# Attention in a hybrid layer: six heads' probabilities turned by VectorE's 32x32 transposes and a DRAM scratch, with gates beside them in single PSUM banks

## The chip, the cores and the metric

The kernel runs on one core of a Trainium2 chip, as one launch. The metric is the device time of the whole kernel in microseconds (us). The engines are named as the profile names them: PE (TensorE, the matrix engine; PEld are its weight loads), DVE (VectorE), ACT (ScalarE), POOL (GpSimd) and SP (SyncE, which here only issues DMAs).

## The reference

One layer over 16 meta tokens and 512 tokens (528 in all) of width 1024: half an FFN, a mixer, half an FFN, a last norm. The mixer adds retention (4 heads) and an attention with selected keys (8 heads of 128), each behind a sigmoid gate. The change lies in the attention and beside it; cut to that, with `selected` standing for a mask that an index of its own makes:

```python
u = rmsnorm(h, mix_norm)
proj = u @ w_in                                  # ..., aq, ak, av, ..., g_ret, g_att
aq = rope(aq.reshape(B, T, 8, 128), pos)
ak = rope(ak.reshape(B, T, 8, 128), pos)
av = av.reshape(B, T, 8, 128)
s = einsum('bqhd,bkhd->bhqk', aq, ak) * 128 ** -0.5
p = softmax(where(selected | meta_and_causal, s, -inf), axis=-1)
ya = einsum('bhqk,bkhd->bqhd', p, av).reshape(B, T, 1024) @ w_att_out
merged = sigmoid(g_ret) * yr + sigmoid(g_att) * ya
h = h + merged @ w_mix_out
```

All is float32.

## The kernel before

**Numbers in two parts.** PE multiplies fp32r operands. A float32 tensor is kept as a high and a low half: `split` (L115 to L118) has ACT copy the high half (L117) and DVE subtract it from the source for the low half (L118). A product is three matmuls, high by high, high by low, low by high (`mm3`, L157). Weights are fetched as `raw` by SP (L133, two buffers) and split into `whi` and `wlo` (three buffers each): a split can start when PE has done with the weights three before.

**Layout.** Activations lie feature by token: 128 features in the partitions, tokens along the free dimension. Scores of one head (`score`, L1964) come query by key: four blocks `prob[j]` of 128 queries in the partitions, with the meta keys and the first 128(j + 1) keys in the free dimension. DVE adds the mask and takes the maximum (L1967), ACT takes the exponential and its sum (L1970), DVE scales to one (`to_one`, L1974 and L1975, tile `pj`). The values are multiplied with the probabilities key by query, so the blocks have to be turned.

**Turning, before.** `transpose_p` has PE transpose the 128x128 blocks with the identity into PSUM (tile `psPT`, 13 blocks at L1988 and a 16-key tail at L1990) and splits each of four key blocks into `pth` and `ptl`. Columns begin at `KQ[kb]`, 512, 400, 272 and 256 of them. `split_rows` makes the tail's stacked rows (`ptail`). `weigh_v` runs 13 matmuls into `psao` (L1536, L1537) and splits the result into the head's part of `vo`.

**The loop over heads.** An iteration h is scores(h), then `proj_q` and `proj_k` of head h + 1 (tiles `psaq`, `psak`; rope by `rope_swap`, whose multiply by sin is POOL's, L1294), the transposes of head h, one gate of 24 matmuls (`wide_gate`: a retention gate, `psgate`, or an attention gate, `psga`, which goes to the DRAM scratch `gd`), and the weighing of head h. Scores of head 0 lie ahead of the loop. Head 7 has no next head, and runs two more gates in that place.

**Order.** Each engine works through its instructions in order. On the engines in `BUSY`, stretches under `manual_schedule` keep the order written; elsewhere a planner with a cost for each instruction sets the order on each engine. DMAs issued by SP, ACT and POOL stand in the queue of that engine among its other instructions. A DMA that waits for data holds what is behind it.

**PSUM.** Single banks come from `sm_tile`, pairs of banks from `mm_tile`. A new tile waits until the last reader of the one that had the place is done.

**Norms.** The sum of squares over features needs a sum over partitions. `folded` adds the upper half of the partitions to the lower and splits; `sum_columns` (L225) multiplies with ones; `rstd_of` takes POOL's power (L252), DVE places the result on diagonals (L283), PE spreads it over the partitions (L266), ACT copies that to SBUF (L267). For the retention heads the same is done by `fold`, `norm_sums`, `norm_diag` and `norm_all` (L1587), hung into other work: `proj(..., ((6, f), ...))` calls f ahead of the sixth weight row's matmuls. `pick(n)` issues n steps of the index selection.

## Time and profile before

| | us |
|---|---|
| median of 3 runs (1516.49 to 1516.9) | 1516.57 |
| the profiled execution, whole | 1517.2 |
| its span, first to last instruction | 1515.4 |

In a row of the profile's timeline stand the start and the duration in us, the engine, the line, the operation, output and inputs by the program's names, the shape, and how many instructions the row joins; in brackets the idle time before it and what ended that. A group row gives the line, the engine, the operation, the shapes and the count, then the busy time in us and the mean in ns, then the idle time before it. A DMA row gives the target, the source, the issuing queue, the count, the KB of each, and the median us from issue to landing. A table of stretches gives the busy us and instruction count of each engine between two times.

### The profile page before, as it was taken

To read this page: it belongs to the slowest core of one execution; us is meant where nothing else is said; L and a number is where in the kernel's file an instruction comes from. 1 tells how busy PE (TensorE), PEld (TensorE's weight loads), DVE (VectorE), ACT (ScalarE), POOL (GpSimd) and SP (SyncE) were. 2 spreads that over 40 slices of the span, in tenths; PEclk is the share of its full clock that TensorE was granted. 3 is DMA by queue.
4 is the path that set the end of the run, shared out by engine and by line. 5 is a ranking of instruction groups with operands and counts; after the bars stand their busy time and mean duration, and the time that the engine had idled before them with its cause. 6 is when DMAs were issued, how large, how long until landed. Compare 5 with 4: busy or idle time off the path is not lost. (4 is left out here: it accounts for less than half of the span.)

```text
span 1515.4 us, 23886 instructions
## 1 busy us (share of the span) xinstructions
PE 1505.2 (99%) x9748; PEld 1368.3 (90%) x9748; DVE 1100.8 (73%) x1710; ACT 727.7 (48%) x1134; POOL 103.2 (7%) x135
## 2 busy tenths in 40 slices
PE   9999999999999999999999999999999999999997
PEld 8999999999988888888888889998888899899996
DVE  4988585786786768678888887665455888586675
ACT  5655263454354444443333357666345445254453
POOL 1000000003101120000000131110001000000000
PEclk9999999999999999999999999999999999999999
DMA  5132323226544444232323242333443223233232
GB/s 169 61 118 89 116 92 112 87 95 202 201 157 162 166 149 151 87 122 86 120 75 97 89 133 75 91 86 105 146 145 113 84 84 112 83 112 112 84 124 85
DMA packets 151741, 173.48 MB, mean 114 GB/s; under 512 B 4944, under 2 KB 123240, under 8 KB 150992
## 3 DMA queue, kind: packets, MB, share of 16 engines
q1 hardware_dynamic: 142992, 151.58, 31.2%
q0 software_dynamic: 3808, 11.38, 2.0%
q10 hardware_dynamic: 4832, 9.00, 1.7%
q8 instruction: 76, 1.25, 0.3%
q14 instruction: 33, 0.27, 0.1%
HBM read 155.94 MB, written 16.01 MB: 113 GB/s over the span
## 5 line engine op out<-in xcount | busy, mean ns | idle before, releaser
L328 ACT ACTIVATE whi<-raw 128x1024 fp32r<-128x1024 f32 (+2 forms) x184 | 169.5, 924 | 128.3 <-PE psd L157 41.6
L329 DVE TENSOR_TENSOR wlo<-raw,whi 128x1024 fp32r<-128x1024 f32 (+2 forms) x184 | 198.5, 1083 | 40.3 <-ACT whi L328 40.3
L157 PE MATMUL psqX<-th,whi 128*128 128x264 f32 (+1 forms) x432 | 122.3, 283 | 0.1
L157 PE MATMUL psqX<-tl,whi 128*128 128x264 f32 (+1 forms) x432 | 122.3, 283 | 0.0
L157 PE MATMUL psqX<-th,wlo 128*128 128x264 f32 (+1 forms) x432 | 122.2, 283 | 0.0
L118 DVE TENSOR_TENSOR wlo<-raw,whi 128x1024 fp32r<-128x1024 f32 (+1 forms) x60 | 73.6, 1226 | 52.1 <-ACT whi L117 51.2
L328 ACT ACTIVATE whi<-wsum 128x1024 fp32r<-128x1024 f32 x72 | 76.3, 1060 | 70.4 <-PE psd L2187 22.0
L117 ACT ACTIVATE whi<-raw 128x1024 fp32r<-128x1024 f32 (+1 forms) x60 | 62.4, 1044 | 85.9 <-PE psat L157 26.6
L329 DVE TENSOR_TENSOR wlo<-wsum,whi 128x1024 fp32r<-128x1024 f32 x72 | 87.8, 1220 | 12.5 <-ACT whi L328 12.5
L157 PEld LDWEIGHTS psqX<-th,whi 128*128 128x128 f32 x432 | 82.1, 190 | 0.4 <-DVE g L544 0.4
L157 PEld LDWEIGHTS psqX<-th,wlo 128*128 128x128 f32 x432 | 82.0, 190 | 0.0
L157 PEld LDWEIGHTS psqX<-tl,whi 128*128 128x128 f32 x432 | 82.0, 190 | 0.0
L157 PE MATMUL psro<-vo,whi 128*128 128x512 f32 x256 | 79.2, 390 | 0.2 <-DVE vo L329 0.2
L157 PE MATMUL psd<-hl,whi 128*128 128x264 f32 x352 | 71.3, 284 | 0.0
L157 PE MATMUL psd<-hh,wlo 128*128 128x264 f32 x352 | 70.7, 283 | 0.0
L157 PE MATMUL psd<-hh,whi 128*128 128x264 f32 x352 | 70.7, 282 | 0.0
L2187 PE MATMUL psd<-wlo,hh 128*128 128x512 f32 (+1 forms) x182 | 69.2, 382 | 0.0
L2187 PE MATMUL psd<-whi,hh 128*128 128x512 f32 (+1 forms) x182 | 69.2, 382 | 0.0
L2187 PE MATMUL psd<-whi,hl 128*128 128x512 f32 (+1 forms) x182 | 69.2, 382 | 0.0
L157 PEld LDWEIGHTS psro<-vo,whi 128*128 128x128 f32 x256 | 48.0, 188 | 10.7 <-DVE vo L329 0.5
L157 PEld LDWEIGHTS psd<-hh,wlo 128*128 128x128 f32 x352 | 54.4, 188 | 0.0
L157 PEld LDWEIGHTS psd<-hh,whi 128*128 128x128 f32 x352 | 54.1, 188 | 0.0
(460 smaller groups left out, 4517.0 us busy)
## 6 DMA issues: line engine op xcount, KB each, us to landing
raw<-in_ffn_w_up_dram SPq DMA_DIRECT2D x22, 1024.0 KB, 5.0
raw<-in_ffn_w_gate_dram SPq DMA_DIRECT2D x21, 1024.0 KB, 5.0
raw<-in_w_in_dram SPq DMA_DIRECT2D x18, 1024.0 KB, 5.0
raw<-in_w_in_dram SPq DMA_DIRECT2D x33, 512.0 KB, 3.5
raw<-in_ffn_w_down_dram SPq DMA_DIRECT2D x24, 512.0 KB, 4.4
w<-in_w_in_dram SPq DMA_DIRECT2D x24, 512.0 KB, 6.9
raw<-in_ffn_w_down_dram SPq DMA_DIRECT2D x12, 768.0 KB, 4.4
raw<-in_w_ret_out_dram SPq DMA_DIRECT2D x8, 1024.0 KB, 4.8
```

The source lines that it names most:

```text
L117: nc.scalar.activation(hi, src, AF.Copy)
L118: eng.tensor_tensor(lo, src, hi.bitcast(F32), ALU.subtract)
L157: nc.tensor.matmul(o, a[:, k, :], b[:, sl], start=first and k == 0 and i == 0, stop=last and k == nk - 1 and i == 2, skip_group_check=onto)
L328: nc.scalar.activation(hi, src, AF.Copy)
L329: return lambda: nc.vector.tensor_tensor(lo, src, hi.bitcast(F32), ALU.subtract)
L2187: nc.tensor.matmul(ps, a[:, bs], m[:, j, cs], start=first and i == 0, stop=last and i == 2)
```

## The change

Heads 1 to 6 no longer use `transpose_p`.

- `turn(h)`: DVE's transpose works on 32x32 squares. Four of them (416, 288, 160 and 512 columns) write the squares of the four blocks to `cross`, and a fifth the 16-key tail to `crosst`. POOL then issues four DMAs to a DRAM scratch `pd` (1 MB a head, two of them in turn), each for 32 partitions: 512 pieces of 512 B, 256 KB. A small DMA takes the tail to `land4`.
- `turned(h)`: SP issues four DMAs from `pd` to `land0` to `land3`, key by query, of 512, 512, 384 and 256 columns: 256, 256, 192 and 128 KB.
- `turned_parts`: the splits into `pth` and `ptl`, now from SBUF.
- `weigh_turned`: the 13 matmuls over 512, 512, 384 and 256 columns; the queries come out in another order, which the last split puts right. It runs one iteration later than before, after the next head's `proj_k`. Iteration 1 therefore weighs no head, and head 6 is weighed in iteration 7.

Beside these heads the gate takes a single bank. The values of heads 4 to 7 are split in iteration 0 (after head 0's weighing) rather than 1, and the tail values of those heads are placed in iteration 4 rather than 3. The `tmp` buffers go from seven to four; `cross` takes the room of the values' raw buffer. For the last retention head `fold` moves from after the second to after the first of two gates, `norm_sums` from the sixth to the fourth weight row of `psak`, and two `pick` calls change. The last norm's column sums take an `mm_tile`, its spread an `sm_tile`.

```diff
--- before.py
+++ after.py
@@ -225,13 +225,12 @@
             nc.tensor.matmul(col[:, 2 * b : 2 * b + 2], f[:, b * P : (b + 1) * P], ones_r[:, :2], start=True, stop=True)
         return col[:, :8].rearrange("p (b j) -> p b j", j=2)[:, :, 0]
 
-    def rstd_folded(ssum, dim, dst, sp, psum):
+    def rstd_folded(ssum, dim, dst, sp, place, psum):
 
         f = tmp().bitcast(F32R)[:, :S]
         for _ in folded(ssum, f, tmp()[:, :S]):
             pass
-        col = psum()
-        yield from rstd_of(sum_columns(f, col), S, dim, dst, sp, psum, P)
+        yield from rstd_of(sum_columns(f, place()), S, dim, dst, sp, psum, P)
 
     def rstd_steps(ssum, n, dim, dst, sp, psum, apart=False):
 
@@ -308,6 +307,8 @@
+    pd = dpool.tile([2, S, 4, P], F32, name="pd")
 
     def gap(p, n):
 
@@ -1819,12 +1820,11 @@
             keep_gate(ps)
             weigh(p, 2)
             weigh(p, 3)
-            pick(1)
+            fold(p)
 
         def last_1(ps):
             keep_gate(ps)
-            fold(p)
-            pick(1)
+            pick(2)
 
         def last_2(ps):
             first_kq.append(ps)
@@ -1839,7 +1839,7 @@
             n = 4 - (h == p)
             more += queries_keys(h) + gates[:n] + outputs(h - 1, beside_outputs(h - 1)) + gates[n:]
         more += steps_of(tiles("gr", w_in, OFF_GR + 2 * P, 2), [proj("psgate", REAL, (), last_0), proj("psgate", REAL, (), last_1)])
-        more += steps_of(tiles("ak", w_in, OFF_AK, 1), [proj("psak", None, ((6, lambda: norm_sums(p)), (7, lambda: norm_diag(p))), last_2)])
+        more += steps_of(tiles("ak", w_in, OFF_AK, 1), [proj("psak", None, ((4, lambda: norm_sums(p)), (7, lambda: norm_diag(p))), last_2)])
         more += steps_of(tiles("aq", w_in, OFF_AQ, 1), [proj("psaq", REAL, ((2, lambda: norm_all(p)), (4, lambda: two_normed_parts(p, 0)), (6, lambda: two_normed_parts(p, 2))), last_3)])
         more += outputs(p, lambda i: pick(2 + (i == 0)))
         more += steps_of(tiles("gr4", w_in, OFF_GR + 4 * P, 1), [proj("psgate", REAL, (), first_kq.append)])
@@ -1906,21 +1906,27 @@
         nc.scalar.activation(t, ps, AF.Sigmoid)
         return t
 
+    crs = ExitStack()
     with pool("ao") as ao:
         vo = [ao.tile([P, AH, S], F32R, tag=f"vo{i}", name="vo") for i in range(2)]
         ao_parts = [(vo[0][:, c, :], vo[1][:, c, :]) for c in range(AH)]
         with pool("at") as at:
-            tp.update(pool=at, bufs=7)
+            tp.update(pool=at, bufs=4)
             cos, sin = rope_tables(1, at)
             gap(at, 32)
             prob = []
             for j in range(4):
-                wj = min(P * (j + 2), T)
+                wj = min(P * (j + 2), T + NM)
                 pj = at.tile([P, wj], F32, tag=f"pj{j}", name=f"pj{j}")
-                if j < 3:
-                    nc.gpsimd.memset(pj[:, NM + P * (j + 1) :], 0.0)
+                nc.gpsimd.memset(pj[:, NM + P * (j + 1) :], 0.0)
                 prob.append(pj)
-            gap(at, 48)
+
+
+            Q0 = [0, 0, P, 2 * P]
+            land = [at.tile([P, S - q0], F32, tag=f"land{kb}", name=f"land{kb}") for kb, q0 in enumerate(Q0)]
+            land.append(at.tile([NM, NM], F32, tag="land4", name="land4"))
+            crosst = at.tile([P, 32], F32, tag="crosst", name="crosst")
+            gap(at, 32)
             tails(at, 64)
             gap(at, 16)
             cq, ck = (Cols(w_in, o_ + P, AH - 1, step=1) for o_ in (OFF_AQ, OFF_AK))
@@ -1980,6 +1986,49 @@
                 for j in (2, 1, 0, 3):
                     score(j, q, k)()
 
+            def part_tiles(kb, n):
+                return [at.tile([P, S - Q0[kb]], F32R, tag=f"pt{c}{kb}", name=f"pt{c}")[:, :n] for c in "hl"]
+
+            def turn(h):
+
+                for j in (2, 1, 0, 3):
+                    m = min(-(-(NM + P * (j + 1)) // 32), 16)
+                    nc.vector.transpose(cross[:, :m, j, :], prob[j][:, : 32 * m].rearrange("p (b k) -> p b k", k=32))
+                nc.vector.transpose(crosst, prob[3][:, S : S + 32])
+                d = pd[h % 2]
+                for a in range(4):
+                    nc.gpsimd.dma_start(d.rearrange("(b i) a c -> a i b c", i=32)[a],
+                                        cross[32 * a : 32 * a + 32].rearrange("p b j c -> p b (j c)"))
+                nc.gpsimd.dma_start(land[4], crosst[96 : 96 + NM, NM:])
+
+            def turned(h):
+                for kb, q0 in enumerate(Q0):
+                    nc.sync.dma_start(land[kb].rearrange("p (a c) -> p a c", a=4),
+                                      pd[h % 2, kb * P : (kb + 1) * P, :, q0 // 4 :])
+
+            def turned_parts():
+                parts = []
+                for kb, q0 in enumerate(Q0):
+                    ph, pl = part_tiles(kb, S - q0)
+                    split(land[kb], ph, pl)
+                    parts.append((ph, pl))
+                split_rows(land[4], tp["p"][:, :NM], "hlh")
+                return parts
+
+            def weigh_turned(h, parts, v):
+
+                ps = mm_tile("psao")[:, :S]
+                for kb, q0 in enumerate(Q0):
+                    vh, vl = (part[:, kb * P : (kb + 1) * P] for part in v[:2])
+                    ph, pl = (part.rearrange("p (a c) -> p a c", a=4) for part in parts[kb])
+                    o = ps.rearrange("p (a c) -> p a c", a=4)[:, :, q0 // 4 :]
+                    if q0 == 0:
+                        (ph, pl), o = parts[kb], ps
+                    for i, (a, b) in enumerate(((vh, ph), (vh, pl), (vl, ph))):
+                        nc.tensor.matmul(o, a, b, start=kb == 0 and i == 0, stop=False)
+                nc.tensor.matmul(ps[:, KQ[4] :], v[2], tp["p"][:TR, :NM], start=False, stop=True)
+                split(*(t.rearrange(f"p ({o}) -> p a j c", a=4, j=4) for o, t in zip(("a j c", "j a c", "j a c"), (ps, *ao_parts[h]))))
+
             def transpose_p():
                 parts = []
                 for kb in range(4):
@@ -1989,8 +2038,7 @@
                     if kb == 3:
                         nc.tensor.transpose(ps[:NM, 0:P], prob[3][:, 4 * P : T], ident)
                     n = S - KQ[kb]
-                    ph = at.tile([P, wide(n)], F32R, tag=f"pth{kb}", name="pth")[:, :n]
-                    pl = at.tile([P, wide(n)], F32R, tag=f"ptl{kb}", name="ptl")[:, :n]
+                    ph, pl = part_tiles(kb, n)
                     if kb == 3:
                         split_rows(ps[:NM, P - NM : P], tp["p"][:, :NM], "hlh")
                     split(ps[:, KQ[kb] :], ph, pl)
@@ -2004,7 +2052,7 @@
 
             def wide_gate(tile=None):
                 if gr.at < gr.n:
-                    gate_acc(KD - gr.n + gr.at, gate(gr, at, wide=True))
+                    gate_acc(KD - gr.n + gr.at, gate(gr, at, wide=tile is None))
                 else:
                     t = gate_a(tile or mm_tile("psga")[:, :S])
                     nc.sync.dma_start(gd[KD + ga.at - 1], t)
@@ -2025,6 +2073,7 @@
                     to_one()
                 vs = split_values(raw, [v[:, :4, :] for v in vo])
                 raw = fetch_values(5, vraw())
+            pend = None
             for h in range(AH):
                 more = h + 1 < AH
                 if h:
@@ -2034,17 +2083,30 @@
                 else:
                     wide_gate(sm_tile("psga"))
                     wide_gate()
-                pt = transpose_p()
-                wide_gate()
-                weigh_v(h, pt, vs[h])
-                if h == 1:
+                if pend is not None:
+                    weigh_turned(h - 1, pend, vs[h - 1])
+                    pend = None
+                if h == 0:
                     with tc.manual_schedule(engines=BUSY):
-                        more_vs = split_values(raw, [v[:, 4:, :] for v in vo])
-                if h == 3:
+                        vs += split_values(raw, [v[:, 4:, :] for v in vo])
+                    vrs.close()
+                    crp = crs.enter_context(pool("cross", 1, side="right"))
+                    cross = crp.tile([P, 16, 4, 32], F32, tag="cross", name="cross")
+                    for j in range(3):
+                        nc.gpsimd.memset(cross[:, 4 * j + 5 :, j, :], 0.0)
+                if 0 < h and more:
+                    turn(h)
+                    wide_gate(sm_tile("psga"))
+                    turned(h)
+                    pend = turned_parts()
+                else:
+                    pt = transpose_p()
+                    wide_gate()
+                    weigh_v(h, pt, vs[h])
+                if h == 4:
                     place_tails(5)
-                    vs += more_vs
-
-        vrs.close()
+
+        crs.close()
 
         mgs = ExitStack()
         mgp = mgs.enter_context(pool("mgp", 1, side="right"))
@@ -2112,7 +2174,7 @@
         RS = slice(0, S)
 
 
-        norm = rstd_folded(ssum3, D, R3, ou, lambda: mm_tile("psn")[:, :S])
+        norm = rstd_folded(ssum3, D, R3, ou, lambda: mm_tile("psn"), lambda: sm_tile("psn"))
         raw0 = load_w(wg2[:, 0 : 2 * P], KD, 2 * P)
         ps0 = [sm_tile("psg") for _ in range(2)]
         for i in range(2):
```

## The prediction

> **What bounds the kernel now.** I read the page's busy shares first, then its chain of waits.
>
> ```profile
> span 1515.4 us, 23886 instructions
> ...
> PE 1505.2 (99%) x9748; PEld 1368.3 (90%) x9748; DVE 1100.8 (73%) x1710; ACT 727.7 (48%) x1134; POOL 103.2 (7%) x135
> ...
> PE 42%; DVE 0%; ACT 0%; issue 0%; POOL 0%; POOLq 0%
> ```
>
> PE works 1505.2 of 1515.4 us, and only PE has a share of the chain that ended last. So the time changes by PE work taken off or added, and by waits put between PE instructions; work on DVE, ACT, POOL and the queues counts only where PE comes to wait for it. Next, the stretches of the attention loop, one head each (PE, PEld, DVE, ACT, POOL, clock, DMA share, GB/s), head 2's and the sum of six:
>
> ```profile
> 936.60:958.90 22.30, 22.30 (x141) 20.26 (x140) 14.56 (x36) 14.73 (x28) 3.92 (x3) 1.00 0.26 72
> ...
> sum 133.90, PE 133.90 PEld 121.57 DVE 88.63 ACT 88.32 POOL 20.58; mean PE 22.32 PEld 20.26 DVE 14.77 ACT 14.72 POOL 3.43
> ```
>
> PE is full at 22.3 us a head. DVE and ACT have over 7 us free, POOL 18, the DMA engines about two thirds. There the change puts its new work.
>
> **Off PE: the transposes.** The timeline shows PE at the end of head 1's loads of k, the 14 transposes, and the gate after them. A matmul's duration overlaps the next one, so I count from start to start.
>
> ```profile
> 927.62 1.58 PE L1988 MATMUL psPT<-ident,pj 128*128 128x128 f32 x13
> ...
> 929.06 0.48 PE L157 MATMUL psgate<-xh,whi 128*128 128x512 f32 x1
> ...
> 929.38 0.39 PE L157 MATMUL psgate<-xl,whi 128*128 128x512 f32 x1
> ...
> 929.61 0.39 PE L157 MATMUL psgate<-xh,wlo 128*128 128x512 f32 x1
> ```
>
> 927.62 to 929.06 is 1.44 us for the transposes, and the first gate matmul takes 0.32 instead of 0.23, so 1.53 us a head. Heads 0 and 7 keep theirs: 6 x 1.53 = 9.2 us off PE. The PSUM bank use of L1988 goes with them.
>
> **Onto PE: wider weighing.** The turned weighing has as many matmuls (13), over 512, 512, 384 and 256 columns in place of 512, 400, 272 and 256.
>
> ```profile
> 934.62 0.39 PE L1536 MATMUL psao<-pth,vo 128*128 128x512 f32 x1
> ...
> 934.85 0.39 PE L1536 MATMUL psao<-ptl,vo 128*128 128x512 f32 x1
> ...
> 935.48 0.34 PE L1536 MATMUL psao<-ptl,vo 128*128 128x400 f32 x1
> ...
> 935.66 0.47 PE L1536 MATMUL psao<-pth,vo 128*128 128x400 f32 x2
> ...
> 935.97 0.29 PE L1536 MATMUL psao<-ptl,vo 128*128 128x272 f32 x1
> ...
> 936.10 0.41 PE L1536 MATMUL psao<-pth,vo 128*128 128x272 f32 x2
> ...
> 936.34 0.28 PE L1536 MATMUL psao<-ptl,vo 128*128 128x256 f32 x1
> ...
> 936.61 0.43 PE L1964 MATMUL psS<-ak,aq 128*128 128x400 f32 x1
> ```
>
> Starts lie 0.23 us apart at 512 columns, 0.18 at 400, 0.13 at 272; 384 columns come between the last two, about 0.175. Three matmuls each: 3 x (0.05 + 0.045) = 0.28 us a head, 6 x 0.28 = 1.7 us. The other PE work only changes places: a turned head is weighed in the next iteration, after the next head's k.
>
> **Two new waits.** In the built programs' instruction order I compared, for every PE instruction, how many PE instructions lie between it and the latest one that its inputs go back to. At two places the change puts a weight split, which waits for a gate's last matmul, ahead of work that PE needs at once. The rows that price them are head 1's in ACT and DVE order:
>
> ```profile
> 932.12 0.65 ACT L117 ACTIVATE ak<-tmp 128x528 fp32r<-128x528 f32 x1 [0.66 <-DVE tmp L1295]
> ...
> 932.83 0.70 DVE L118 TENSOR_TENSOR ak<-tmp,ak 128x528 fp32r<-128x528 f32 x1
> ...
> 933.82 0.38 ACT L117 ACTIVATE pth<-psPT 128x256 fp32r<-128x256 f32 x1 [1.06 <-DVE ptail L1370]
> ...
> 934.24 0.42 DVE L118 TENSOR_TENSOR ptl<-psPT,pth 128x256 fp32r<-128x256 f32 x1 [0.51 <-ACT pth L117]
> ...
> 934.64 1.06 ACT L117 ACTIVATE whi<-raw 128x1024 fp32r<-128x1024 f32 x1 [0.44 <-PE psgate L157]
> ...
> 935.74 1.23 DVE L118 TENSOR_TENSOR wlo<-raw,whi 128x1024 fp32r<-128x1024 f32 x1 [1.07 <-ACT whi L117]
> ```
>
> Before, the halves of k (ak) and of the last probability block (pth, ptl) are made first; then whi starts 0.02 us after PE has left the gate (934.62), and wlo after it.
>
> (1) Iteration 1. It has no head to weigh, so scores(2) follow gate(1) directly, and ACT now has whi ahead of ak's high half, DVE wlo ahead of its low half. From the gate's end whi runs to +1.08, wlo to +2.35, ak's low half to +3.08. The first score matmul needs the high half alone and covers 0.18: a stall of 2.9 us. Queued behind whi on ACT are the sigmoid and all of softmax(2); PE meanwhile has proj_q(3) and proj_k(3), so nothing else is late.
>
> (2) Iteration 0. Head 0 is not turned, but its last block's pth and ptl now stand behind the same pair: whi to +1.08, wlo to +2.35, ptl to +2.8. The weighing reaches that ptl 1.72 us after its start (936.34 - 934.62): a stall of 1.1 us. Before, that weighing took
>
> ```profile
> 912.12 0.39 PE L1536 MATMUL psao<-pth,vo 128*128 128x512 f32 x1
> ...
> 914.28 1.90 PE L1964 MATMUL psS<-ak,aq 128*128 128x400 f32 x12
> ```
>
> 2.16 us, against head 1's 1.99: 0.17 of waiting is there already, so +0.9. Both together cost +3.8 us; the bounds are 0 (the gate's weights freed in time after all) and 6 (a splitting pair more in front).
>
> **The last norm.** rstd_folded's column sums move to an mm bank and its spread to an sm bank. Now:
>
> ```profile
> 1172.30 0.40 PE L266 MATMUL psn<-tmp,ones_r 128*128 128x512 f32 x1
> ...
> 1172.74 0.60 ACT L267 ACTIVATE R<-psn 128x512 f32<-128x512 f32 x1 [4.90 <-PE psn L266]
> ...
> 1173.39 0.50 PE L157 MATMUL psu<-xh,whi 128*128 128x512 f32 x1 [0.69 <-ACT R L267]
> ...
> 1173.73 0.39 PE L157 MATMUL psu<-xl,whi 128*128 128x512 f32 x1
> ```
>
> psu waits until ACT has emptied the bank: it starts 1.09 us after psn rather than 0.23, and its second matmul comes 0.34 later rather than 0.23. In the new order psu doesn't depend on that copy: -1.0 us; bounds -1.0 and 0. The fold in last_0 and the earlier norm_sums move DVE and ACT work of the last retention head forward by a step; no PE work changes, PE's weights there are loaded ahead, and I take 0, within -0.3 and +0.5 (bounds: an ACT or DVE piece as long as ak's low half, 0.70, less what covers it).
>
> **The trip and its cover.** Per turned head DVE gets five 32x32 transposes of 1408 columns; nothing like it is in the trace. By wlo's 1.2 ns a column it's 1.7 us (bounds: 0.8 and 3.4, half and double). DVE then is busy 16.3 us of some 21: hidden. POOL gets five issues, SP four:
>
> ```profile
> L1126 POOL DMA_DIRECT2D vst<-part x12 | 8.5, 712 | 77.8 <-DVE part L1154 59.9 <-ACT part L1202 10.9 <-DVE part L1192 6.9
> ```
>
> ```profile
> q1 hardware_dynamic: 142992, 151.58, 31.2%
> ...
> vst<-part POOLq DMA_DIRECT2D x12, 512.0 KB, 5.4
> ...
> sa<-gd ACTq DMA_DIRECT2D x8, 256.0 KB, 4.0
> ...
> vraw<-vst SPq DMA_DIRECT2D x4, 256.0 KB, 15.1
> ...
> vd<-rest POOLq DMA_DIRECT2D x6, 128.0 KB, 2.1
> ...
> rqk<-fs SPq DMA_DIRECT2D x2, 256.0 KB, 5.6
> ```
>
> vst has as many pieces (512, of 1 KB) as one write of pd (of 512 B): 0.71 us to issue, so five take 3.6 of POOL's 18 free. Landing: 2.1 (vd) to 5.4 (vst). Now the times, from the start of a head's scores (936.61 for head 1's next, 914.28 for head 0's next):
>
> ```profile
> 930.01 1.33 POOL L1294 TENSOR_TENSOR tmp<-tmp,sin 128x528 f32<-128x528 f32 x1 [4.50 <-ACT tmp L1292]
> ...
> 942.00 0.49 DVE L1975 TENSOR_SCALAR pj<-pj,stat 128x528 f32<-128x528 f32 x1
> ```
>
> Probabilities are final at +5.9 (942.49 - 936.61), turned at about +8. Of the four writes the last stands behind k's rope multiply on POOL, which ends at +17.1 (931.34 - 914.28) less the 1.5 of transposes: issued by +16.3, landed by +18.4 to +21.7. SP then loads 256, 256, 192 and 128 KB: two to three loads' time of 4.0 to 5.6, so +26 to +31; DVE's low halves (0.7 each at 512 columns) are done 1 to 2 us later. PE weighs that head after the next head's k, one period (21.0) plus 13.3 (927.62 - 914.28) = +34.3. So 1 to 6 us to spare: I cost it at 0. If the cover is gone, each us late is a us of PE in each of six heads.
>
> [...]
>
> **Sum.** -9.2 + 1.7 + 2.9 + 0.9 - 1.0 = -4.7 us: span 1515.4 to 1510.7. The profiled run took 1517.2, 1.8 more than its span; the median of the three runs is 1516.57, which I take as the start: 1511.9.
>
> **Rivals.**
> (A) The waits don't come or are covered: -9.2 + 1.7 - 1.0 = -8.5, 1508.1. For it: PE is full now with the same splits; against: both orders are fixed in the program. 12%.
> (B) k is late at each head. k's low half ends 3.1 us before its scores (936.61 - 933.53); taking transposes out and weighing earlier leaves 1.8, and 1.7 of DVE's turning and 1.4 of POOL issues can stand ahead of it: 0 to 1.3 us in each of five scores. At 0.8 it gives 4.0, 1515.9. For it: POOL's rope multiply is in that chain; against: POOL has waited 4.5 us before it. 17%.
> (C) Slower: the trip is late. q1's packets take 31.2% x 16 x 1515.4 / 142992 = 53 ns at about 1 KB. A turned head adds 2048 written and 2048 read, 256 an engine: 7 us (half a KB, half the time) to 13.5 of 21, on a share of 0.26 to 0.36. At 0.6 the trip fits, at 0.95 loads take as long as vraw's 15.1. Then pth waits on ACT with softmax and weight splits behind it in order, and the weights behind the loads on SP come late. It decides from 0.8 us a head (4.7 / 6). At 2 us a head: 1511.9 + 12 = 1523.9. 26%. [...]
> (D) It doesn't do what it says: PE keeps a transpose per head elsewhere. The order shows 28 left of 112, so I give it nothing.
>
> **How the numbers follow.** My forecast has 45%, with a range of its own of 1509 to 1514.5. What this kernel can tell from no change is 0.2%, 3.0 us: faster is below 1513.5, slower above 1519.6. Faster: 0.41 of the forecast's 0.45, A's 0.12, 0.03 of B: 0.56. Slower: 0.24 of C and 0.02 of B: 0.26. The rest, 0.18, is the same. Range: below, A less half a us; above, C up to 1.7 us a head: 1507.5 to 1522.
>
> **What would show it.** Right: no psPT in heads 1 to 6; stretches of about 21 us from scores(3) to scores(7); a gap of 2.5 to 3 us ahead of scores(2), released by DVE's ak, and of about 1 us ahead of head 0's last block; psu 0.23 us after psn. Wrong: PE waiting at psao for ptl in heads 1 to 6 or at psgate, psaq, psak for wlo (C), at psS for ak from head 3 on (B), or a DMA share over 0.8 there.

## The result, and the profile after

| | before | after |
|---|---|---|
| median, us (9 runs each) | 1516.86 (1516.49 to 1517.49) | 1512.7 (1511.5 to 1513.67) |
| the profiled execution, us | 1517.2 | 1512.66 |
| its span, us | 1515.4 | 1510.8 |

The ratio is 0.9974, with a 95% interval of 0.9965 to 0.9982: 4.2 us faster, forecast 1511.9. The profiled span is 4.6 us shorter. One of the nine executions had a granted clock of 1.000 and took 1511.5 us; the others had 0.997 or 0.998 and took 1512.66 us or more. The sum came out near with several terms wrong, on both sides of it, as will be seen. First the page's first lines and its chain of waits:

```profile
span 1510.8 us, 23879 instructions
...
PE 1498.6 (99%) x9664; PEld 1361.2 (90%) x9664; DVE 1113.5 (74%) x1740; ACT 729.9 (48%) x1134; POOL 122.2 (8%) x169
...
PE 97%; DVE 1%; ACT 1%; issue 1%; DMA 0%; POOL 0%; POOLq 0%; DVEq 0%; ACTq 0%
```

PE's busy time fell by 6.6 us and the span by 4.6, so PE now stands still 2.0 us longer than before. DVE and ACT have shares in the chain that they didn't have (the chain of before could be followed over 42% of its span only). PE's waits in the whole program (engine, tile and line, releaser: us in total, times, longest us):

```profile
PE psao L1537 <- DVE ptl L118: 1.9, 1, 1.9
PE psg L653 <- DVE idle L621: 1.5, 1, 1.5
PE psS L1970 <- ACT ak L117: 1.5, 1, 1.5
PE psS L1970 <- DVE ak L118: 0.9, 1, 0.9
```

The second was there before. The others are the two waits of the forecast, the first at head 0, the last two in front of `scores(2)`. A stretch of one turned head, from scores to scores:

```profile
979.90:1001.00 21.10, 21.10 (x126) 18.83 (x125) 16.79 (x41) 15.05 (x27) 7.26 (x10) 1.00 0.70 201
```

A head takes 21.10 us rather than 22.3, PE is full, and the DMA share (the last number but one) is 0.70 where it was 0.26. Here is the wait at head 0:

```profile
909.22 1.22 DVE L118 TENSOR_TENSOR vo<-vraw,vo 128x1024 fp32r<-128x1024 f32 x1
...
911.50 2.36 DVE L118 TENSOR_TENSOR wlo<-raw,whi 128x1024 fp32r<-128x1024 f32 x2
...
913.78 0.42 DVE L118 TENSOR_TENSOR ptl<-psPT,pth 128x256 fp32r<-128x256 f32 x1
...
914.25 0.39 PE L1537 MATMUL psao<-ptl,vo 128*128 128x256 f32 x1 [1.85 <-DVE ptl L118]
```

Ahead of `ptl` DVE makes the low halves of two weights (`x2`, 2.36 us), and before those the second of two low halves of the values (`vo<-vraw`, 1.22 each). From 905.41 to 914.20, the end of `ptl`, DVE is busy for 8.61 of 8.79 us: it is behind with its list, where the forecast had one split that waits for the gate's end (910.49). And the wait at `scores(2)`:

```profile
933.25 0.71 DVE L1296 TENSOR_TENSOR tmp<-tmp 128x528 f32<-128x528 f32 x1 [0.70 <-POOL tmp L1295]
...
934.98 1.06 ACT L117 ACTIVATE whi<-raw 128x1024 fp32r<-128x1024 f32 x1 [3.18 <-PE psgate L157]
...
935.95 0.63 ACT L117 ACTIVATE ak<-tmp 128x528 fp32r<-128x528 f32 x1
...
936.07 1.23 DVE L118 TENSOR_TENSOR wlo<-raw,whi 128x1024 fp32r<-128x1024 f32 x1 [2.12 <-ACT whi L117]
...
937.21 0.70 DVE L118 TENSOR_TENSOR ak<-tmp,ak 128x528 fp32r<-128x528 f32 x1
```

k's rope, the source of `ak`, was done at 933.96. ACT stood idle for 3.18 us until PE had left the gate, made `whi`, and only then the high half of `ak`; DVE stood idle for 2.12 us, waiting for that `whi`, with the low half of `ak` behind it. Third, something that the forecast hadn't: three stretches of 3.41 us around the first wait (the columns are those of the stretches above; the third number from the end is the granted clock).

```profile
912.43:915.84 3.41, 1.59 (x11) 1.59 (x12) 2.15 (x4) 2.36 (x4) 1.28 (x1) 1.00 0.61 169
915.84:919.25 3.41, 3.41 (x14) 3.02 (x13) 3.07 (x17) 2.93 (x8) 0.00 (x0) 0.50 0.51 139
919.25:922.66 3.41, 3.41 (x17) 2.78 (x16) 2.99 (x10) 0.45 (x2) 0.00 (x0) 1.00 0.00 0
```

After a stretch in which PE worked 1.59 of 3.41 us (each matmul counted to its modelled end), it runs at a clock of 0.50 for one more, and the PE column has it busy for 3.41 of 3.41 us, while 512-column matmuls start 0.43 us apart (917.41, 917.84, 918.27) rather than 0.23. By the clock that is 1.7 us lost, half of 3.41, an estimate; by the starts it's 1.55: from the first score to the seventh `psaq` it takes 5.03 us (914.62 to 919.65), and 3.48 in before (914.28 to 917.76). No list of waits shows it. Last, two norms. Before, around the last retention head's (timeline of PE):

```profile
853.73 0.40 PE L157 MATMUL psaq<-xh,wlo 128*128 128x512 f32 x1
854.16 0.47 PE L1587 MATMUL psn<-tmp,ones_r 128*128 128x512 f32 x1
854.47 0.39 PE L157 MATMUL psaq<-xh,whi 128*128 128x512 f32 x1
...
859.95 0.46 PE L157 MATMUL psro<-vo,whi 128*128 128x512 f32 x1
860.65 0.50 PE L157 MATMUL psro<-vo,whi 128*128 128x512 f32 x1 [0.23 <-DVE vo L329]
```

and after, there and at the last norm:

```profile
853.00 0.39 PE L157 MATMUL psaq<-xh,wlo 128*128 128x512 f32 x1
853.23 0.39 PE L1588 MATMUL psn<-tmp,ones_r 128*128 128x512 f32 x1
853.45 0.39 PE L157 MATMUL psaq<-xh,whi 128*128 128x512 f32 x1
...
1169.72 0.40 PE L265 MATMUL psn<-tmp,ones_r 128*128 128x512 f32 x1
1169.95 0.40 PE L157 MATMUL psu<-xh,whi 128*128 128x512 f32 x1
```

In after the starts are 0.23 us apart at both norms. Before, they were 0.43 and 0.31 around `psn` and 0.70 between the two `psro`: 0.20 + 0.08 + 0.47, and 0.11 at the next `psro`, together 0.87 us that are gone. Put together, start to start (us of the span):

| where | us |
|---|---|
| six heads, 22.32 to 21.09 each (the mean of four heads that wait for nothing) | -7.4 |
| wait in front of `scores(2)` | +2.9 |
| wait at head 0's last block | +2.0 |
| half clock behind it, as half of 3.41 | +1.7 |
| last retention head's norm | -0.9 |
| last norm | -1.0 |
| up to the first `psrq`, 394.57 to 393.83 | -0.7 |
| behind PE's last matmul | -1.0 |
| sum | -4.4 |

The spans differ by 4.55; rounding, the 1.55 of the starts in place of 1.7, and pieces of 0.1 us make the rest. The last two rows above the sum are not PE work of the change. The first matmul behind the first FFN (`psqX`) starts at 84.71 us in before and 84.16 in after, and anywhere from 83.94 (e11_short) to 85.17 (e3_order) in kernels that are alike up to there, so -0.7 is what one execution differs from another. It goes with the time at which the clock record first grants the full clock: 6.66 us into the span in before, 4.48 in after, and 7.57, the latest of all, in e3_order; that this is the cause was not tested. For the -1.0, see what stays open.

### The profile page after: what moved, and what is told of

The parts are those of the page before. It is cut to its first block, busy times and chain, and to the rows that moved or that the text cites. A ratio compares the mean times of both kernels' runs of the same rounds, so it can differ in the third digit from the quotient of the medians.

```text
span 1510.8 us, 23879 instructions
## 1 busy us (share of the span) xinstructions
PE 1498.6 (99%) x9664; PEld 1361.2 (90%) x9664; DVE 1113.5 (74%) x1740; ACT 729.9 (48%) x1134; POOL 122.2 (8%) x169
## 3 DMA queue, kind: packets, MB, share of 16 engines
HBM read 161.05 MB, written 22.30 MB: 121 GB/s over the span
## 4 chain that ended last, share of the span: by engine, by line
PE 97%; DVE 1%; ACT 1%; issue 1%; DMA 0%; POOL 0%; POOLq 0%; DVEq 0%; ACTq 0%
PE psqX L157 14%; PE psd L157 8%; PE psd L2249 8%; PE psqY L157 7%; PE psrg L157 6%; PE psro L157 6%; PE psvX L1181 4%; PE psqZ L157 3%; PE psrk L157 3%; PE psu L157 3%; PE psrq L157 3%; PE psga L157 3%; PE psat L157 3%; PE psmo L157 3%; PE psak L157 3%; PE psaq L157 3%
## 5 line engine op out<-in xcount | busy, mean ns | idle before, releaser
L118 DVE TENSOR_TENSOR wlo<-raw,whi 128x1024 fp32r<-128x1024 f32 (+1 forms) x60 | 73.6, 1228 | 28.3 <-ACT whi L117 27.4
```

Source lines behind the costliest of these rows:

```text
L118: eng.tensor_tensor(lo, src, hi.bitcast(F32), ALU.subtract)
```

## The experiments

The kernel before gave 1516.72, 1517.07 and 1516.73 us as median of three groups of runs; every ratio is to the runs of before on the same chip.

### One half of the change each

e1_norms is before with the edits of the norms alone (`fold`, `norm_sums`, the `pick`s, and the two banks of the last norm). e2_turn is after without them. Their diffs are the hunks shown above.

> The kernel before with the norms' edits alone: fold and norm_sums of the last retention head earlier with their picks, and the last norm's column sums in an mm bank, its spread in an sm bank. Heads are transposed by PE as before. In the trace of the changed kernel PE's waits of 0.87 us at the last retention head (206, 82, 466 and 114 ns) and of 0.97 us at psu are gone. Theory: they belong to these edits, and the time falls by 1.8 us, 1516.9 to 1515.1. Rival: the earlier 0.87 went with the new order of the scheduler around the turned heads, not with the fold; then the time falls by 1.0 us, to 1515.9, and psro waits as before. Second rival: run-to-run differences only, 1516.9.

> The changed kernel without the norms' edits: the turned heads alone. Theory: the two parts add up, 1512.7 + 1.8 = 1514.5, with both waits of the norms back and the three losses at the heads unchanged (2.1 us ahead of head 0's last block, 2.9 us ahead of scores(2), 3.4 us at half clock after the first). Rival (the norms' gain needs nothing from these edits): 1512.7.

e1_norms: 1515.11 us, ratio 0.999 (0.9981 to 0.9999). e2_turn: 1515.45, ratio 0.9994 (0.9985 to 1.0003). e2_turn's waits of PE:

```profile
PE psao L1538 <- DVE ptl L118: 1.9, 1, 1.9
...
PE psS L1972 <- ACT ak L117: 1.5, 1, 1.5
PE psS L1972 <- DVE ak L118: 0.9, 1, 0.9
PE psu L157 <- ACT R L267: 0.7, 1, 0.7
PE psro L157 <- DVE vo L331: 0.2, 1, 0.2
```

e1_norms came out as expected. e2_turn has the waits at the heads, the half clock too, and the norms' two waits are back. Its median is 1.0 above the theory's 1514.5; the profiled execution was its fastest, 1514.35, and the eight with a granted clock of 0.996 or 0.997 took 1515.12 to 1517.98, the three with 0.998 1514.35 to 1515.13. The rival's 1512.7 for it, which has the norms' edits give nothing, falls. So the heads' part, with 9.2 us of transposes taken off, is worth 1.3 us as it stands, which its interval can't tell from nothing; the norms' part, of which the forecast had only one bank, is worth 1.6.

### The order of the weight splits

e3_order is after with edges in the planner's order: a weight split that waits for a gate may not stand ahead of the halves that PE needs first, and neither may the gate's sigmoid on ACT.

```diff
-        split(v, hv, lv, eng)
+        with ExitStack() as order:
+            for i in behind:
+                order.enter_context(tc.issue_after(i))
+            split(v, hv, lv, eng)
...
+                    if h == 1:
+                        behind.extend(i.ins for i in made["p"])
+                    if h == 2:
+                        behind.extend(i.ins for i in ready)
+                    if h == 1:
+                        late.append(made["k"][0].ins)
                     wide_gate(sm_tile("psga"))
+                    behind.clear()
+                    late.clear()
...
+                    if h == 0:
+                        late.append(made["p"][0].ins)
                     wide_gate()
+                    late.clear()
```

Here `made["p"]` is the last `pth` and `ptl` of head 0, `ready` the halves of the next k, and `late` does for the sigmoid what `behind` does for the split. e4_order1 has only the edges of iteration 1, those for `scores(2)`.

> The changed kernel with order edges alone, no work added or removed: gate(1)'s weight split and gate(0)'s sigmoid behind head 0's last pth and ptl; gate(2)'s weight split and gate(1)'s sigmoid behind k(2)'s halves. Theory: both waits were in-order queueing behind splits that wait for a gate's end, and the half clock (1.7 us lost) follows PE's first wait: 1512.7 - 2.0 - 2.9 - 1.7 = 1506.1, PE without a gap at both places, clock 0.999 or more. Rival on the second wait (k(2) is late because turn(1)'s DVE and POOL work stands ahead of its rope): only the first wait goes, 1509.0. Rival on the clock (it dips by itself, from the new mix of work): 1507.8, with a record of half clock near the start of scores(1).

> The changed kernel with the order edges of iteration 1 alone; head 0's last block still waits behind two weight splits. Theory: 1512.7 - 2.9 = 1509.8, the wait of 2 us and the half clock after it still there. Rival (k late by turn(1)'s work): 1512.7. Rival on the clock (the dip needs two waits close together, or comes from something else): 1508.1, the first wait there and no record of half clock.

e3_order: 1508.2 us, ratio 0.9944 (0.9931 to 0.9956), 2.1 above the theory's 1506.1. e4_order1: 1508.82, ratio 0.9953 (0.9941 to 0.9966), with two of its five runs 2.3 and 2.7 us above that median, at a granted clock of 0.998 where the other three had 0.999. In e3_order the wait at `scores(2)` is down to 0.23 us and there is no half clock; but at head 0 some is left. DVE and PE there:

```profile
910.22 1.22 DVE L118 TENSOR_TENSOR vo<-vraw,vo 128x1024 fp32r<-128x1024 f32 x1
...
912.49 1.22 DVE L118 TENSOR_TENSOR wlo<-raw,whi 128x1024 fp32r<-128x1024 f32 x1
913.63 0.42 DVE L118 TENSOR_TENSOR ptl<-psPT,pth 128x256 fp32r<-128x256 f32 x1
...
914.11 0.38 PE L1544 MATMUL psao<-ptl,vo 128*128 128x256 f32 x1 [0.78 <-DVE ptl L118]
```

One of the two `wlo` is still ahead, and the values' low halves too. That wait, 0.9 us by the starts, is one part of the 2.1 us above the theory; another 1.0 us lies ahead of the attention, where the profiled execution of e3_order reaches `psqX` at 85.17 and that of after at 84.16. Between the medians, taking out most of the two waits and their half clock brings 4.5 us (1512.7 less 1508.2). e4_order1 keeps the whole wait of head 0 (1.9 us in its profile), yet that profile has no half clock behind it, and its time is nearer to the rival without one (1508.1) than to the theory (1509.8): whether the wait brings the half clock isn't fixed.

### The split of the values

e5_values is e3_order with the values of heads 4 to 7 split behind head 0's weighing; e6_values_only is after with that alone, without the edges.

```diff
-                if h == 0:
-                    with tc.manual_schedule(engines=BUSY):
-                        vs += split_values(raw, [v[:, 4:, :] for v in vo])
...
                     pt = transpose_p()
                     wide_gate()
                     weigh_v(h, pt, vs[h])
+                if h == 0:
+                    with tc.manual_schedule(engines=BUSY):
+                        vs += split_values(raw, [v[:, 4:, :] for v in vo])
```

> The kernel with the order edges (e3_order), and the split of the values of heads 4 to 7 moved from ahead of head 0's transposes to behind head 0's weighing, in the same iteration. In e3_order PE still waited 0.94 us for head 0's last ptl: DVE, which takes its work in order, had two low halves of values (1.22 us each) and one weight low half ahead of it. Theory: the values' splits, moved into iteration 0 by the change, make that rest: the wait falls to 0.2 or less, 1508.2 - 0.8 = 1507.4. Rival (the weight low half ahead of ptl is enough to hold it): 1508.2.

> The changed kernel with the values' split moved behind head 0's weighing, and no order edge. Theory: head 0's wait of 2.0 us came from DVE's backlog in iteration 0, values and weight splits together; moving the values lets the scheduler put ptl ahead: the wait falls to 0.2, and with it the half clock that follows it in the profile (1.7 us); the 2.9 us at scores(2) stay: 1512.7 - 1.8 - 1.7 = 1509.2. Rival (the two weight splits alone hold ptl, as the prediction had it): a wait of 1.1 us is left, 1510 to 1511.5. Rival on the clock (the dip is no effect of that wait): 1510.9 with a half-clock record left.

e5_values: **1507.2 us (1506.97 to 1507.86), ratio 0.9935 (0.9922 to 0.9949)**, the best of all, 9.9 us under before on the same chip. DVE and PE at head 0:

```profile
912.17 0.42 DVE L118 TENSOR_TENSOR ptl<-psPT,pth 128x256 fp32r<-128x256 f32 x1
...
912.50 2.35 DVE L118 TENSOR_TENSOR wlo<-raw,whi 128x1024 fp32r<-128x1024 f32 x2
...
912.64 0.39 PE L1544 MATMUL psao<-ptl,vo 128*128 128x256 f32 x1
```

Both `wlo` now come after `ptl`, and PE doesn't wait. In e6_values_only the same happens without any edge, so at head 0 it was the place of the values' split that put the weights in front. e6_values_only took 1511.84 us, ratio 0.9962 (0.9949 to 0.9974), more than the 1509.2 of the theory. Its stretches around `scores(2)`:

```profile
930.36:933.77 3.41, 1.73 (x7) 0.92 (x5) 1.30 (x3) 2.30 (x3) 0.44 (x1) 1.00 0.60 167
933.77:937.18 3.41, 2.75 (x11) 2.74 (x12) 2.06 (x10) 2.89 (x4) 1.28 (x1) 0.50 0.70 213
937.18:940.59 3.41, 3.41 (x12) 2.82 (x11) 2.46 (x12) 3.36 (x13) 0.00 (x0) 0.50 0.64 191
```

The first wait is gone, but behind the second, which had no half clock in after, there now are 6.82 us of it. The wait theory held, the price of what follows the wait didn't. One of the five executions had a granted clock of 0.999, as without a half clock, and took 1509.47 us, near the theory's 1509.2; the other four had 0.997 and took 1511.35 to 1512.13.

### When a wait brings the half clock

e8_waits and e11_short make the wait in front of the scores longer by a chosen amount: DVE multiplies k by one n times before its halves are made (e8_waits: on e3_order, n = 8, 10, 12, 16, 20 for heads 3 to 7; e11_short: on e5_values, n = 2 to 6).

```diff
+                for _ in range(slow[0]):
+                    nc.vector.tensor_scalar(y, y, 1.0, None, ALU.mult)
                 made["k"] = split(y, k[0], k[1])
```

> e3_order with k of heads 3 to 7 multiplied by one 8, 10, 12, 16 and 20 times on DVE (0.49 us each, one after the other) ahead of its split, so that PE waits ahead of five scores, for some 2, 3, 4, 6 and 8 us. It asks whether a wait of PE brings a half-clock stretch, as the 3.4 us at 0.5 that began 1.5 us after the wait of 2.0 us in the changed kernel's profile. Theory: a wait of 2 us or more, in one piece, is followed by a stretch at 0.5 within a few us, here at most or all of the five. Rival (the dip is by chance, or from something else at head 0): none of the five, or one without relation to a wait. The time by the waits alone would be 1508.2 + 23 = 1531, and up to 1.7 more for each dip.

> e5_values with k of heads 3 to 7 multiplied by one 2, 3, 4, 5 and 6 times on DVE (0.49 us each) ahead of its split, so that PE waits ahead of five scores for some 0.5 to 4 us. In the traces so far a half-clock record lasts 3.41 us or a multiple, records within one run begin whole multiples of 3.41 us apart (27.3 = 8 of them), and where PE waited 1.9 us within one such window, once a half-clock record followed (changed kernel), once not (the third wait of e8_waits: 1.9 us in the window ahead of the one that was idle for 3.4). Theory: the clock of a window is set by the window before: halved when PE idled in it for more than some 2 us, whatever the wait's whole length. So waits of 2 us and less bring none or one by where the window's edge falls, and those above 3.5 us all bring one. Rival (the length of the wait alone decides, from 2 us on): a record after each wait over 2 us.

e8_waits took 1548.5 us and e11_short 1515.28, one run each. The theory's 1531 and half clock on top was too low for e8_waits: its listed waits ahead of the scores alone came to 29.2 us (28.3 for the high half of k, 0.9 for the low), not 23. Its five long ones last 3.5, 3.5, 4.8, 7.8 and 9.5 us, with half clock behind them for 3.41, 3.41, 3.41, 6.82 and 10.24 us. The stretches around the first of these:

```profile
955.26:958.67 3.41, 0.49 (x2) 0.22 (x2) 2.28 (x3) 3.36 (x5) 0.00 (x0) 1.00 0.24 53
958.67:962.08 3.41, 3.41 (x14) 3.41 (x15) 1.60 (x9) 1.57 (x6) 0.00 (x0) 0.50 1.05 344
962.08:965.49 3.41, 3.41 (x17) 2.84 (x16) 3.06 (x12) 3.41 (x10) 0.00 (x0) 1.00 0.34 86
```

and around the only half clock of e11_short:

```profile
1018.48:1021.89 3.41, 1.06 (x5) 0.38 (x3) 1.84 (x2) 3.03 (x4) 0.00 (x0) 1.00 0.09 33
1021.89:1025.30 3.41, 3.41 (x15) 3.40 (x16) 1.60 (x9) 2.90 (x7) 0.00 (x0) 0.50 0.93 297
```

In e8_waits the five half-clock records start 27.31, 27.30, 27.31 and 30.72 us apart, which is 8, 8, 8 and 9 times 3.413: the granted clock changed only at edges of stretches of 3.41 us, which follow a beat of their own. The clock record gives the beat also where no stretch of the work was slow: in before the full clock lasts from 6.66 to 1511.93 us, 441 times 3.413; in after the clock changes at 4.48, 915.84, 919.25 and 1506.35 us, 267, 1 and 172 times 3.413 apart. What parts the cases is how long PE is idle within one stretch, here reckoned from the starts (matmuls of 512 columns start 0.23 us apart, where the PE column counts each to its modelled end at 0.39). Full-clock stretches with 2.02 (after), 2.1 (e6_values_only), 2.3 (e2_turn), 2.5 (e7_late), 2.8 (e8_waits and e11_short) and 3.2 us or more (e8_waits) of idle PE were each followed by a slow one. Those with 1.6 (after and e11_short), 1.92 (e8_waits), 1.96 (e2_turn) and 1.99 (e9_wide) were not.

So in these runs the length of a wait doesn't decide, and the rival of e11_short, which went by it, falls. The wait of 2.2 us in e4_order1 is longer than the 2.0 of after at the same place, but a stretch's edge at 913.37 cuts it, and no more than 1.4 us lie in one stretch. The waits at `scores(2)` are the same 1.6 and 1.2 us in after and in e6_values_only; in after an edge at 936.32 parts them into 1.3 and 1.6, in e6_values_only 2.1 us fall into one stretch. In the cases shown a slow stretch was followed by another where PE was still idle for part of it (0.66 us by the PE column in e6_values_only), and by a full one where PE was busy throughout (3.41 of 3.41 us in after, e8_waits and e6_values_only's second). The waits of e11_short stayed at 2.8 us and less, so that long ones all bring a slow stretch is shown by e8_waits alone.

### How thin the cover of the trip is

e10_unused is before with the norms' edits, the values split as in e5_values, and the whole trip made and loaded, but not used: the heads are transposed by PE and weighed as before. It asks whether the trip itself costs PE anything.

```diff
+                if 0 < h and more:
+                    pt = transpose_p()
+                    turn(h)
+                    wide_gate()
+                    turned(h)
+                    weigh_v(h, pt, vs[h])
```

e7_late is e3_order with the four writes of `pd` behind POOL's rope multiply of the next k, where POOL's order had some of them ahead of it:

```diff
-                for a in range(4):
+                with tc.issue_after(sins[-1]):
+                  for a in range(4):
```

> The kernel before with the norms' edits, the values' split as in e5_values, and the whole trip of heads 1 to 6 beside it (DVE's transposes, the writes, the loads), whose result isn't used: PE transposes and weighs as before the change. Theory: the trip costs PE nothing where it is covered, so this runs like the kernel before with the norms' edits (e1_norms), 1515.1, and 6 x 1.25 = 7.5 us above e5_values, 1514.7. Rival (DVE, POOL and DMA work makes k or the weights late, 0.5 to 1.5 us a head): 1518 to 1524.

> e3_order with the four writes to the scratch of each turned head put behind k's rope multiply on POOL by order edges; no work added. The last write was behind it already, so the trip ends by three issues of 0.67 us later, 2 us, at most. Theory: the cover left over (1.2 to 6.1 us between the first low half and its weighing, in e3_order) takes most of it; PE waits 0 to 1 us in some of six heads: 1508.2 to 1512. Rival (the cover is thin at all heads, since the splits are queued behind other work that the scheduler fits to it): over 2 us a head, 1520 or more.

e10_unused: 1513.84 us, ratio 0.998 (0.9971 to 0.9989), not above e1_norms (1515.11) but 1.3 below it. A head in it:

```profile
936.60:958.90 22.30, 22.30 (x140) 20.24 (x140) 16.21 (x41) 14.69 (x28) 6.49 (x8) 1.00 0.56 156
```

The same 22.30 us as before with twice the DMA share (0.56, before 0.26): the trip as such costs PE nothing here. The trip's DMAs in after, writes and loads (us from issue to landing last in a row):

```profile
pd<-cross POOLq DMA_DIRECT2D x24, 256.0 KB, 3.3
...
land<-pd SPq DMA_DIRECT2D x12, 256.0 KB, 4.3
...
land<-pd SPq DMA_DIRECT2D x6, 192.0 KB, 4.4
...
land<-pd SPq DMA_DIRECT2D x6, 128.0 KB, 3.3
```

and the widest of DVE's groups of squares in after (busy us, mean ns of one, then idle):

```profile
L1996 DVE STREAM_TRANSPOSE cross<-pj 128x512 f32<-128x512 f32 x6 | 4.2, 694 | 0.1
```

e7_late: 1520.43 us, ratio 1.0023 (1.0014 to 1.0032), 12.2 more than e3_order. Its waits of PE:

```profile
PE psao L2039 <- DVE ptl L118: 4.9, 8, 0.9
PE psao L2039 <- ACT pth L117: 1.5, 1, 1.5
```

PE now waits at `psao` for `ptl` eight times and for `pth` once in the weighing of turned heads, with 6.82 us of half clock on top (the clock record of its trace); against before on the same chip it loses 3.4 us, where e3_order gains 8.5. This is the slower rival's sign, a trip that is late.

But the late writes aren't all of the cause. Counted from the scores of the next head, head 1's last write left POOL 2.1 us later than in e3_order and landed 3.6 later. SP, however, issued the loads 9.4 us later (10.8 us after these scores in place of 1.4), because two weight loads that wait for DVE (`raw`, 935.65 to 942.66) now stand ahead of them in its order. In head 4 the first load lands at 8.5 us after the scores, as in e3_order (8.7), but ACT makes `pth` 3.8 us later: the high half of q, which waits 2.2 us for its rope, stands in front. So the edges on POOL made the planner change the order on SP and ACT too, and how much of the 12.2 us two microseconds alone would cost isn't shown. The cover itself can be read: in e3_order 1.2 to 6.1 us lie between the first low half and its weighing.

### The gate's bank

e9_wide is e5_values with the gates beside turned heads in pairs of banks, as before:

```diff
-                    wide_gate(sm_tile("psga"))
+                    wide_gate()
```

> e5_values with the gates beside the turned heads in pairs of banks again, as before the change. With the transposes gone from between, such a gate takes the pair that k's projection has just left, and waits until DVE's rope multiply has read it: in the changed kernel that read ended 3.1 us after the projection (929.4 to 932.5), and the weighing that lies between takes 2.3 us. Theory: this part of the change keeps PE from a wait of 0.8 us at the gates of heads 2 to 6: 1507.2 + 4.0 = 1511.2. Rival (the read comes in time, or the wait falls where PE would wait anyway): 1507.2.

e9_wide: 1513.53 us, ratio 0.9982 (0.9973 to 0.9992), 6.3 more than e5_values. The new wait:

```profile
PE psga L161 <- DVE tmp L1298: 5.9, 5, 1.8
```

Five gates wait for the place that q's or k's projection had, until DVE's rope has read it. With the transposes gone only a weighing lies between them, which is too short: in after the weighing of head 1 takes 2.3 us (951.13 to 953.42), and the rope's read of iteration 1 ends 3.0 us behind the projection (the gate after it starts at 929.53, the read ends at 932.54). Without the single bank some two thirds of the gain go: 3.2 us are left of 9.9, each against before on the same chip. Expected were 4.0 us, and the gates wait 6.7 by the starts.

## Why the prediction was right, and where it wasn't

- **Transposes off, weighing wider.** -9.2 + 1.7 = -7.5 us; measured -7.4, in stretches of 21.1 us. Right, for the mechanism and the size.
- **Wait (1), `scores(2)`.** Forecast 2.9 us, measured 2.9, with the order foreseen: `whi`, `wlo`, then `ak`. e3_order takes it away.
- **Wait (2), head 0.** Forecast +0.9, measured +2.0. The step that failed is "the same pair", one split of weights ahead of `ptl`, which put the end of `ptl` 2.8 us behind the gate. There were two `wlo` and before them two low halves of the values, DVE was behind with its list, and `ptl` ended 3.7 us behind the gate (914.20 less 910.49). The change's description has these values split after head 0's weighing; in the code they stand ahead of head 0's transposes. That is what pushed `ptl` back: e6_values_only moves them and the wait is gone.
- **The half clock.** No step of the forecast had it: a wait was priced at its own length. It made up 1.7 us in after (1.55 by the starts), and the missing price is shown by e6_values_only and e8_waits. The granted clocks of the single runs show that it isn't even the same from run to run of one kernel.
- **The last norm.** -1.0 for the bank: measured -1.0 (`psu` 0.23 us behind `psn`).
- **The fold and the sums, moved.** "I take 0" was wrong: -0.87, outside the bounds of -0.3 and +0.5, because the gaps of 0.08 to 0.47 us in before's list of starts weren't looked for. e1_norms and e2_turn show the norms' part at 1.6 and 2.8 us between the medians (1516.72 less 1515.11; 1515.45 less 1512.7), its rows at 1.84. The second holds what half clocks differ between the executions.
- **The trip, at nothing.** Right: e10_unused. Of its terms, DVE's turning was 2.28 us a head, not 1.7 (five groups' means; the bounds held), the writes landed in 3.3 by their median but up to 6.9 (forecast 2.1 to 5.4), the loads in 2.6 to 6.4 (4.0 to 5.6). The forecast of 1 to 6 us to spare met 1.2 to 8.0 from the first `ptl`'s end to the weighing.
- **Rivals.** (A) no waits: it didn't happen, but e3_order and e5_values show what it would be, 1508.2 and 1507.2 against its 1508.1. (B) k late each head: not here; 0.8 to 1.9 us of slack ahead of the scores, in one head almost none. (C) trip late: not here. That its 12 us at 2 us a head are near e7_late's 12.2 is chance: there half clock is 3.4, the heads lose from nothing to some 4 us, and the order on SP and ACT has its part. Its count of packets was too high as well. Of the 2048 written and 2048 read for a head, the traces have 256 and 1280: the writes move in packets of 4 KB, the whole loads in 2 KB, and only the two narrow loads in the pieces of 384 and 256 B. The DMA share was 0.55 to 0.70. (D): no transposes by PE in heads 1 to 6.

So 1511.9 against 1512.7 is a sum in which +1.1 (head 0) and +1.7 (clock) were missing on one side, and -0.9 (norm), -1.0 (end) and -0.7 (start, by which executions differ) on the other. The transposes, the weighing, `scores(2)` and the last norm were foreseen; that the rest nearly cancels is luck.

**What stays open.** The 1.0 us behind PE's last matmul, which starts at 1507.46 in before and at 1503.94 in after. From there to the span's end it's 7.9 us before and 6.9 after. Up to the landing of the last output the two are alike (5.8 and 5.9 us); from there to the last instruction it's 2.1 and 1.0. It is 1.0 shorter in every kernel that has the trip, e10_unused too, and not in e1_norms; why, no run tells, and it's most of the 1.3 by which e10_unused undercuts e1_norms. From how much idling in a stretch on the half clock comes isn't shown: the nearest cases, 1.99 us without it (e9_wide) and 2.02 with it (after), are one execution each, and the PE column (1.58 busy in e9_wide's, 1.59 in after's) can't part them. What late writes alone would cost stays open too. Turning head 0 as well wasn't tried: `cross` has no room beside the raw values.

## What to carry to other kernels

When PE work is taken out, look in the new instruction order of ACT and DVE for what now stands ahead of the operands PE needs next: a split that waits for a gate's end cost 2.9 us here, a list of splits that DVE wasn't through with 2.0, together over half of what the turning saved, and a few order edges with one block of code moved gave most of it back. Price a wait of PE with the half clock that may follow (here it came behind 2.0 us of idling in one stretch and took 1.55 us by the starts), and look at starts, not at listed waits alone. An order edge can move more than it names: after e7_late's edges on POOL the loads on SP and the splits on ACT came late as well, so read the new order on every engine before a loss is put down to the edge's own delay.

## What the hardware showed that was not expected

- In every case with PE idle for 2.02 us (after) to 3.2 us or more (e8_waits) inside one 3.41 us stretch the whole next stretch ran at half clock (0.50); with 1.99 us (e9_wide) it didn't, nor with a wait of 2.2 us that a stretch's edge cut (e4_order1). It shows in the granted clock and the starts (0.43 us apart in after, not 0.23), not in PE's busy time (3.41 of 3.41 us there).
- In e8_waits, waits of 3.5 and 4.8 us brought 3.41 us of it, 7.8 brought 6.82, 9.5 brought 10.24: one, two and three whole stretches.
- DVE's transpose of 32x32 squares took 0.69 us for 128x512 float32, as long as a low half of that size (0.68 for `ptl`).
- POOL's writes of 512 pieces of 512 B each moved in 64 packets of 4 KB. Loads in packets of 384 B and 256 B landed in 4.4 us (192 KB) and 3.3 us (128 KB), next to 4.3 for 256 KB in packets of 2 KB: more time for each KB in the shorter packets (23 and 26 ns, next to 17).
